# The first feed-forward's input products with output features on the partitions

## The chip, the cores and the metric

The program runs on one core of a Trainium2 chip. The core has a matrix engine (TensorE, in the rows PE for its products and PEld for its weight loads), a vector engine (VectorE, DVE), an activation engine (ScalarE, ACT), GpSimd (POOL) and SyncE (SP), which here only starts transfers. Each engine takes its instructions strictly in the order of the program; engines wait for each other through semaphores. The metric is the device time of one execution in microseconds.

## What is computed

Two transformer blocks on one sequence of 256 tokens, width 2048. The change touches the first block's feed-forward, whose hidden width D_FF is 5632 and whose input product makes 2 x 5632 features. They go through a causal convolution over time with three taps for each feature before the gate is applied:

```python
def rms_norm(x, g):
    xf = x.astype(jnp.float32)
    y = xf * lax.rsqrt(jnp.mean(xf * xf, axis=-1, keepdims=True) + NORM_EPS)
    return (y * g.astype(jnp.float32)).astype(x.dtype)

def conv_glu_ffn(h, w_up, cw, cb, w_down):
    u = causal_depthwise_conv(h @ w_up, cw, cb)      # (256, 2048) @ (2048, 11264), 3 taps
    a, gate = jnp.split(u, 2, axis=-1)
    return (jax.nn.silu(gate) * a) @ w_down

        h = rms_norm(x, ffn_norm_g[l])               # first_block
        x = x + conv_glu_ffn(h, w_up[l], ffn_conv_w[l], ffn_conv_b[l], w_down[l])
```

Around it: the first block's attention with its convolution branch, before; the product with `w_down`, a norm, and the whole second block (two attentions, a gated feed-forward), after.

## The kernel before

All products are float32 in three parts. An operand x is rounded to xh, and the remainder x - xh is xl; a weight gives hi and lo in the same way. A product is xh·hi + xh·lo + xl·hi.

**Items.** The weights come from memory in items of 512 KB: two k-tiles (128 rows each of the contraction) by 512 columns. Each item runs through a pipeline. `load_upto` lets SP start its transfer into a `raw` tile (four of them). `split_upto` (L272) lets ACT round it into `hi` (L281) and DVE subtract it into `lo` (L282); four `hi` and four `lo` tiles exist, `AHEAD` is 3. Then PE uses it. `run_items` writes the program item by item: first the split of the item three places ahead, then this item's products in two halves, one k-tile each. So the instruction `hi` of item i+3 stands on ACT where item i is begun, and it reuses the tile of item i-1.

**Side work.** After each half item `pump` (L242) steps the queues. `urgent` has the rate 0.5: of the functions pushed to it, one is written into the program after every second half, that is one for each item. When a function is written, all its instructions stand on their engines in that place. A function that reads something late therefore holds back whatever stands behind it on the same engine, the splits of later items among it.

**A group** (L201) is all items that make 512 output columns; with a contraction of 2048 it has 8 items. Its mode `xst` (L192) keeps the activations stationary: for each of two halves of the tokens, xh and xl are the weights that PE loads, and 512 columns of hi or lo are the moving operand. The result stands in two PSUM banks, with the tokens on the partitions. An item is 12 products of 512 columns.

**The first feed-forward** is 22 groups: for each of 11 blocks one of the gate columns, one of the up columns. After a group's last product `ffn1_post` (L1045) evicts: `take` copies both banks to `e` tiles on ACT, multiplied by `rstd`, the norm's factor, one for each partition (token). It then pushes for each half b of the 512 features a function `f`: `turn4` transposes four squares of 128 on PE so that features stand on partitions, and `taps3` makes the three taps, the first on ACT (L1036) and four instructions for the other two on DVE (L1041); in a gate group Silu follows (L1055). For an up group a function `g` follows for each half: the product with the gate (DVE, L1061) and the split into `sh` and `sl` for the next product (`split_into`, ACT L418, DVE L419).

**The activations** reach this stage by `turn_split` (L395), which transposes the residual stream and writes xh and xl into separate tiles of the common pool "U" (NU = 63 tiles of 128x512), two k-tiles in each.

Of the kernel before, what the change touches and what calls it, by code (L numbers as in the profile page):

```python
# [17 lines left out]
F32 = mybir.dt.float32  # L18
# [7 lines left out]
P = 128  # L26
# [8 lines left out]
NU = 63  # L35
# [39 lines left out]
class Pipe:  # L75


    def __init__(self):
        self.q = deque()
        self.later = []  # L80
# [26 lines left out]
class Acts:  # L107


    def __init__(self, pipe):  # L110
        self.d = {}
        self.pipe = pipe if callable(pipe) else lambda kt: pipe

# [10 lines left out]
def body(tc, A, out, stop=None, dbg=None):  # L124
# [76 lines left out]
    def group(w, c0, n, kts, X, post, nk=2, before=None, mode=xst, parts=None, tail=None):  # L201
# [33 lines left out]
        for j in range(nch):  # L235
            ld = chunk_loads(w, kts[j * nk], nk, parts or [(c0, n)])
            add(ld, nk * n, mk(j), post=(lambda: post(st["acc"])) if j == nch - 1 else None,
                before=before if j == 0 else None)

# [155 lines left out]
    def turn_split(X, kt, src, c0, gain=None):  # L395

        b = turn4(src, c0)
        hi, lo = U("xh", F32R), U("xl", F32R)
        h, l = two(hi), two(lo)
# [68 lines left out]
    xT = Acts(urgent)  # L468
# [505 lines left out]
    xT2 = Acts(urgent)  # L974
# [54 lines left out]

    def taps3(src, y, f0):  # L1030
# [14 lines left out]
    def ffn1_post(blk, gate):  # L1045
        def post(acc):
            e = take(acc, rstd)
            for b in range(2):
                st = {}

                def f(b=b, st=st):
                    y = st["y"] = U("yf")
                    taps3(turn4(e, b * T), y, (44 if gate else 0) + 4 * blk + 2 * b)
                    if gate:
                        act.activation(y, y, AF.Silu)  # L1055
                        sil[b] = y
                urgent.push(f)

                def g(b=b, st=st):
                    y = st["y"]  # L1060
                    dve.tensor_tensor(y, y, sil.pop(b), op=ALU.mult)  # L1061
                    split_into(hidT, 4 * blk + 2 * b, y)
                if not gate:
                    urgent.push(g)
        return post

    w_up = w2d("w_up")
    for blk in range(11):
        group(w_up, DFF + blk * 512, 512, allk, xT2, ffn1_post(blk, True))
        group(w_up, blk * 512, 512, allk, xT2, ffn1_post(blk, False))  # L1070

    xT3 = Acts(urgent)
# [402 lines left out]
    xT4 = Acts(urgent)  # L1475
# [124 lines left out]
```

## Time and profile before

| | |
|---|---|
| runs of the kernel | 2857.2, 2854.13, 2855.75 us |
| their median | 2855.75 us |
| the profiled execution's own time | 2856.26 us |
| its span, first to last instruction | 2854.5 us |
| PE busy | 2824.9 us, 99% |
| DVE busy | 1636.0 us, 57% |
| ACT busy | 1424.5 us, 50% |
| mean granted clock of TensorE | 0.996 of full speed |

Busy times overlap, since the engines run side by side; idle time of one engine matters only where another waits for it. Matmuls are pipelined: a row's duration is longer than the distance between the starts of neighbours. The stage that the change rewrites lies between about 420 and 923 us of the span.

### The profile page before, as it was taken

What the parts mean: (1) busy time and instruction counts of PE and PEld (TensorE: products, weight loads), DVE (VectorE), ACT (ScalarE), POOL (GpSimd) and SP (SyncE); (2) the same over time, 40 slices, a digit from 0 to 9 for tenths busy, and PEclk for the clock granted to TensorE, in tenths of its full rate; (3) what the DMA queues carried; (4) which work ended last, traced back from release to release, by engine and by line L of the source; (5) the groups of instructions that cost most, each with busy time, mean ns of one, the idle gap of its engine ahead of it and who ended that gap; (6) DMA issues with size and microseconds to landing.
All of it is one profiled execution on the core that took longest, in us unless ns stands there. A gap on an engine that the chain in (4) does not pass through costs nothing.

```text
span 2854.5 us, 34904 instructions
## 1 busy us (share of the span) xinstructions
PE 2824.9 (99%) x13031; PEld 2332.6 (82%) x13031; DVE 1636.0 (57%) x2488; ACT 1424.5 (50%) x2068; POOL 35.7 (1%) x65
## 2 busy tenths in 40 slices
PE   8998999999999999999999999999999999999998
PEld 7886778888888888888888888888888888888887
DVE  6986766666566555565555455555555454554444
ACT  6556555555555444565543555554454444444443
POOL 1201000000000000000000000000000000000000
PEclk9998999999999999999999999999999999999999
DMA  8753336656665566554466655665566666666664
GB/s 233 239 163 106 111 104 185 191 180 191 190 185 188 195 193 196 173 177 121 142 203 195 178 164 169 175 199 188 186 186 189 191 188 190 190 186 195 198 198 159
DMA packets 279578, 513.01 MB, mean 180 GB/s; under 512 B 21222, under 2 KB 46738, under 8 KB 279408
## 3 DMA queue, kind: packets, MB, share of 16 engines
q1 hardware_dynamic: 272256, 502.86, 57.9%
q0 software_dynamic: 4624, 7.13, 0.9%
q8 instruction: 102, 1.67, 0.2%
q10 hardware_dynamic: 2528, 0.79, 0.1%
q14 instruction: 68, 0.56, 0.1%
HBM read 505.45 MB, written 5.24 MB: 179 GB/s over the span
## 4 chain that ended last, share of the span: by engine, by line
PE 97%; DVE 1%; ACT 1%; DMA 0%; issue 0%; SPq 0%; DVEq 0%
PE acc L164 89%; PE tr L391 2%; PE ms L164 1%; PE o L164 1%; PE s L164 1%; DMA raw<-in_w_in 0%; PE ds L164 0%; PE mo L164 0%; PE pt L807 0%; PE do L164 0%; PE hid L164 0%; DVE lo L282 0%; ACT hi L281 0%; PE pt L809 0%; PE pt L808 0%
## 5 line engine op out<-in xcount | busy, mean ns | idle before, releaser
L282 DVE TENSOR_TENSOR lo<-raw,hi 128x1024 fp32r<-128x1024 f32 (+3 forms) x956 | 1153.3, 1211 | 1009.7 <-ACT hi L281 989.0
L281 ACT CAST hi<-raw 128x1024 fp32r<-128x1024 f32 (+3 forms) x956 | 989.8, 1040 | 877.9 <-PE acc L164 817.4
L164 PE MATMUL acc<-hi,xh 128*128 128x512 f32 (+2 forms) x3200 | 1260.7, 394 | 2.0 <-ACT xh L405 2.0
L164 PE MATMUL acc<-hi,xl 128*128 128x512 f32 (+2 forms) x3200 | 1241.3, 388 | 0.5 <-DVE xl L407 0.5
L164 PE MATMUL acc<-lo,xh 128*128 128x512 f32 (+2 forms) x3200 | 1239.5, 387 | 0.0
L164 PEld LDWEIGHTS acc<-hi,xl 128*128 128x128 f32 x3200 | 601.3, 188 | 124.0 <-DVE xl L407 1.0
L164 PEld LDWEIGHTS acc<-hi,xh 128*128 128x128 f32 x3200 | 601.8, 188 | 118.5 <-ACT xh L405 2.3
L164 PEld LDWEIGHTS acc<-lo,xh 128*128 128x128 f32 x3200 | 602.3, 188 | 115.4 <-DVE lo L282 0.5
L164 PE MATMUL acc<-hi,sh 128*128 128x512 f32 x480 | 192.1, 400 | 9.9 <-ACT sh L590 9.9
L164 PE MATMUL acc<-hi,sl 128*128 128x512 f32 x480 | 188.0, 392 | 0.0
L164 PE MATMUL acc<-lo,sh 128*128 128x512 f32 x480 | 187.6, 391 | 0.0
L164 PEld LDWEIGHTS acc<-hi,sh 128*128 128x128 f32 x480 | 90.8, 189 | 27.6 <-ACT sh L590 10.3
L164 PEld LDWEIGHTS acc<-hi,sl 128*128 128x128 f32 x480 | 90.5, 188 | 19.6 <-DVE sl L594 0.2
L164 PEld LDWEIGHTS acc<-lo,sh 128*128 128x128 f32 x480 | 90.9, 189 | 17.6
L526 DVE SCALAR_TENSOR_TENSOR y<-u,cols,y 128x255 f32<-128x255 f32 (+14 forms) x240 | 96.3, 464 | 0.0
L1041 DVE SCALAR_TENSOR_TENSOR yf<-tr,cols,yf 128x254 f32<-128x254 f32 (+1 forms) x176 | 72.6, 475 | 29.3 <-ACT yf L1036 29.3
L1036 ACT ACTIVATE yf<-tr,cols 128x256 f32<-128x256 f32 x88 | 44.8, 560 | 33.7 <-PE tr L391 33.7
L802 ACT ACTIVATE p<-p,mx 128x256 f32<-128x256 f32 x64 | 28.6, 448 | 57.9 <-DVE mx L796 57.9
L164 PE MATMUL acc<-hi,ymh 128*128 128x512 f32 x128 | 49.8, 389 | 0.0
L164 PE MATMUL acc<-lo,ymh 128*128 128x512 f32 x128 | 49.8, 389 | 0.0
L164 PE MATMUL acc<-hi,yml 128*128 128x512 f32 x128 | 49.8, 389 | 0.0
L428 ACT ACTIVATE e<-acc,rstd 128x512 f32<-128x512 f32 x54 | 36.8, 690 | 24.1 <-PE acc L164 24.1
(314 smaller groups left out, 1429.3 us busy)
## 6 DMA issues: line engine op xcount, KB each, us to landing
raw<-in_w_in SPq DMA_DIRECT2D x216, 512.0 KB, 3.7
raw<-in_w_up SPq DMA_DIRECT2D x176, 512.0 KB, 3.9
raw<-in_w_down SPq DMA_DIRECT2D x88, 512.0 KB, 4.7
raw<-in_w_ffn_gate SPq DMA_DIRECT2D x88, 512.0 KB, 4.4
raw<-in_w_ffn_up SPq DMA_DIRECT2D x88, 512.0 KB, 4.0
raw<-in_w_ffn_down SPq DMA_DIRECT2D x88, 512.0 KB, 4.0
raw<-in_w_out SPq DMA_DIRECT2D x64, 512.0 KB, 3.7
raw<-in_w_in SPq DMA_DIRECT2D x64, 256.0 KB, 3.6
```

The lines of the kernel that those rows point to most:

```text
L164: pe.matmul(o, l, r, start=start, stop=stop, skip_group_check=True)
L281: act.copy(it.hi[:, c], it.raw[:, c])
L282: dve.tensor_tensor(it.lo[:, c], it.raw[:, c], it.hi[:, c].bitcast(F32), op=ALU.subtract)
L391: pe.transpose(b[:, kk * T + t * P: kk * T + (t + 1) * P], src[t][:, c:c + P], ident)
L428: act.activation(u[:, :n], acc[t][:, :n], AF.Copy, scale=scale[:, t:t + 1])
L526: dve.scalar_tensor_tensor(y2[:, kk, s:], u2[:, kk, :T - s], w, y2[:, kk, s:], op0=ALU.mult, op1=ALU.add)
L802: act.activation(dst, dst, AF.Exp, bias=nmx, scale=-1.0, accum_out=sums)
L1036: act.activation(y2[:, kk], t2[:, kk], AF.Identity, scale=c(2), bias=col("ffn_conv_b", f))
L1041: dve.scalar_tensor_tensor(y2[:, kk, s:], t2[:, kk, :T - s], col("ffn_conv_w", k * 88 + f), y2[:, kk, s:], op0=ALU.mult, op1=ALU.add)
```

## The change

Only the 22 groups of the first feed-forward get another form, `groupT`. The weights are now stationary: each 128 columns of hi and of lo are loaded into PE, and the activations move. `turn_split` writes xh and xl of a k-tile side by side into one 512-column piece (`X.wide`) of a double tile with a pool of its own (8 of them; NU falls to 47). For hi the moving operand is this piece, xh beside xl, 512 columns; for lo it is xh alone, 256 columns. The output has features on the partitions. It takes four banks, one for each 128 features ("quarter" q): columns 0 to 255 hold hi·xh + lo·xh, columns 256 to 511 hold hi·xl. Groups use two sets of four banks in turn.

The eviction of a quarter stands directly behind its last product: ACT copies the second half of the bank, DVE adds the first. No transposes remain. Since the tokens are now on the free axis, `rstd` is needed as a row for all partitions; `rstd_row` makes it once as `rT`, with a product of `avg` and a diagonal. When both quarters of a half are evicted, a function `f` is pushed: multiply by `rT`, taps, and Silu (gate) or the gate's product with the split (up), all in one function.

```diff
-NU = 63
+NU = 47
...
+    def groupT(w, c0, X, post):
+        st = {}
+        nch = KT // 2
+        par = turn_banks[0] % 2
+        turn_banks[0] += 1
+
+        def mk(j):
+            def f(hi, lo, half):
+                if j == 0 and half == 0:
+                    st["b"] = [psA.tile([P, 512], F32, name=nm("acc"), tag="acc")
+                               for _ in range(4)] if par == 0 else \
+                        [bank("acc") for _ in range(3)] + \
+                        [psO.tile([P, 512], F32, name=nm("acc"), tag="o")]
+                for q in (2 * half, 2 * half + 1):
+                    o = st["b"][q]
+                    for kk in range(2):
+                        kt = 2 * j + kk
+                        c = slice(kk * 512 + q * P, kk * 512 + (q + 1) * P)
+                        xh = X.get(kt)[0]
+                        mm(o, hi[:, c], X.wide[kt], start=j == 0 and kk == 0)
+                        mm(o[:, :T], lo[:, c], xh, stop=j == nch - 1 and kk == 1)
+                    if j == nch - 1:
+                        post(q, o)
+            return f
...
     def turn_split(X, kt, src, c0, gain=None):
...
+            hl = big.tile([P, 1024], F32R, name=nm("hl"), tag="X2", bufs=8)
+            h4 = hl.rearrange("p (k s c) -> p k s c", k=2, s=2)
+            h, l = h4[:, :, 0], h4[:, :, 1]
+            for kk in range(2):
+                X.wide[kt + kk] = hl[:, kk * 512:(kk + 1) * 512]
...
+    def rstd_row():
+        d = U("rd")
+        for t in range(2):
+            dve.tensor_scalar(d[:, t * P:(t + 1) * P], ident, rstd[:, t:t + 1], 1024.0,
+                              op0=ALU.mult, op1=ALU.mult)
+        b = bank("rT")
+        mm(b[:, :T], avg, d[:, :T], start=True, stop=True)
+        act.copy(rT, b[:, :T])
...
     def ffn1_post(blk, gate):
-        def post(acc):
-            e = take(acc, rstd)
-            for b in range(2):
-                st = {}
-
-                def f(b=b, st=st):
-                    y = st["y"] = U("yf")
-                    taps3(turn4(e, b * T), y, (44 if gate else 0) + 4 * blk + 2 * b)
-                    if gate:
-                        act.activation(y, y, AF.Silu)
-                        sil[b] = y
-                urgent.push(f)
-
-                def g(b=b, st=st):
-                    y = st["y"]
+        st = {}
+
+        def post(q, o):
+            if blk == 0 and gate and q == 0:
+                rstd_row()
+            b, kk = divmod(q, 2)
+            if kk == 0:
+                st[b] = U("e")
+            e = two(st[b])
+            act.copy(e[:, kk], o[:, T:])
+            dve.tensor_tensor(e[:, kk], o[:, :T], e[:, kk], op=ALU.add)
+            if kk == 0:
+                return
+
+            def f(b=b):
+                e, y = st.pop(b), U("yf")
+                dve.tensor_tensor(two(e), two(e), rT.unsqueeze(1).broadcast_to([P, 2, T]),
+                                  op=ALU.mult)
+                taps3(e, y, (44 if gate else 0) + 4 * blk + 2 * b)
+                if gate:
+                    act.activation(y, y, AF.Silu)
+                    sil[b] = y
+                else:
                     dve.tensor_tensor(y, y, sil.pop(b), op=ALU.mult)
                     split_into(hidT, 4 * blk + 2 * b, y)
-                if not gate:
-                    urgent.push(g)
+            urgent.push(f)
...
-        group(w_up, DFF + blk * 512, 512, allk, xT2, ffn1_post(blk, True))
-        group(w_up, blk * 512, 512, allk, xT2, ffn1_post(blk, False))
+        groupT(w_up, DFF + blk * 512, xT2, ffn1_post(blk, True))
+        groupT(w_up, blk * 512, xT2, ffn1_post(blk, False))
```

The other `Acts` that are filled by `turn_split` in these shapes (`xT`, `xT3`, `xT4`) are also made with `wide=True`; their groups keep their form.

**The order of ACT and DVE.** ACT before, from the end of an up group: `e` is the eviction, `hi` a weight split, `yf` the taps, `sh` the split of the hidden values.

```order
L428 ACTIVATE e_4647<-acc_4481,rstd 128x512
L428 ACTIVATE e_4649<-acc_4482,rstd 128x512
L281 CAST hi_4651<-raw_4579 128x1024
L1036 ACTIVATE yf_4671<-tr_4672,cols 128x256 x2
L281 CAST hi_4683<-raw_4597 128x1024
L418 CAST sh_4702<-yf_4671 128x512
L281 CAST hi_4706<-raw_4615 128x1024
L1036 ACTIVATE yf_4724<-tr_4725,cols 128x256 x2
L281 CAST hi_4736<-raw_4633 128x1024
L418 CAST sh_4755<-yf_4724 128x512
L281 CAST hi_4759<-raw_4655 128x1024
```

ACT now, the same place; lines are numbered anew, L314 is the weight split.

```order
L1107 COPY e_4756<-acc_4585 128x256
L1107 COPY e_4756<-acc_4586 128x256
L1107 COPY e_4769<-acc_4587 128x256
L1107 COPY e_4769<-acc_4588 128x256
L1088 ACTIVATE yf_4778<-e_4756,cols 128x256 x2
L458 CAST sh_4787<-yf_4778 128x512
L314 CAST hi_4791<-raw_4684 128x1024
L1088 ACTIVATE yf_4817<-e_4769,cols 128x256 x2
L458 CAST sh_4826<-yf_4817 128x512
L314 CAST hi_4830<-raw_4706 128x1024
```

Before, each `yf` and each `sh` had a `hi` in front of it. Now the whole sequence of a half stands between two `hi`, and the first half's directly behind the evictions.

DVE before, at the same group: L1061 is the gate's product, `lo` the weight split.

```order
L282 TENSOR_TENSOR lo_4652<-raw_4579,hi_4651 128x1024
L1041 SCALAR_TENSOR_TENSOR yf_4671<-tr_4672,cols,yf_4671 128x255 x2
L1041 SCALAR_TENSOR_TENSOR yf_4671<-tr_4672,cols,yf_4671 128x254 x2
L282 TENSOR_TENSOR lo_4684<-raw_4597,hi_4683 128x1024
L1061 TENSOR_TENSOR yf_4671<-yf_4671,yf_4495 128x512
L419 TENSOR_TENSOR sl_4703<-yf_4671,sh_4702 128x512
L282 TENSOR_TENSOR lo_4707<-raw_4615,hi_4706 128x1024
L1041 SCALAR_TENSOR_TENSOR yf_4724<-tr_4725,cols,yf_4724 128x255 x2
L1041 SCALAR_TENSOR_TENSOR yf_4724<-tr_4725,cols,yf_4724 128x254 x2
L282 TENSOR_TENSOR lo_4737<-raw_4633,hi_4736 128x1024
L1061 TENSOR_TENSOR yf_4724<-yf_4724,yf_4526 128x512
L419 TENSOR_TENSOR sl_4756<-yf_4724,sh_4755 128x512
```

DVE now, behind the four additions of the eviction; L1114 is the scaling by `rT`, L1121 the gate's product.

```order
L1114 TENSOR_TENSOR e_4756<-e_4756,rT 128x512
L1093 SCALAR_TENSOR_TENSOR yf_4778<-e_4756,cols,yf_4778 128x255 x2
L1093 SCALAR_TENSOR_TENSOR yf_4778<-e_4756,cols,yf_4778 128x254 x2
L1121 TENSOR_TENSOR yf_4778<-yf_4778,yf_4570 128x512
L459 TENSOR_TENSOR sl_4788<-yf_4778,sh_4787 128x512
L315 TENSOR_TENSOR lo_4792<-raw_4684,hi_4791 128x1024
L1114 TENSOR_TENSOR e_4769<-e_4769,rT 128x512
L1093 SCALAR_TENSOR_TENSOR yf_4817<-e_4769,cols,yf_4817 128x255 x2
L1093 SCALAR_TENSOR_TENSOR yf_4817<-e_4769,cols,yf_4817 128x254 x2
L1121 TENSOR_TENSOR yf_4817<-yf_4817,yf_4605 128x512
L459 TENSOR_TENSOR sl_4827<-yf_4817,sh_4826 128x512
L315 TENSOR_TENSOR lo_4831<-raw_4706,hi_4830 128x1024
```

Before, a `lo` stood between the taps and the gate's product of each half. Now everything from the scaling to `sl` stands together for each half, and one `lo` behind it.

PE before, early in the up group: the last three products of a k-tile, a set of transposes (`tr`) of the gate group's `e`, and the next item.

```order
L164 MATMUL acc_4482<-hi_4417,xh_3759 128x512
L164 MATMUL acc_4482<-lo_4418,xh_3759 128x512
L164 MATMUL acc_4482<-hi_4417,xl_3760 128x512
L391 MATMUL tr_4496<-ident,e_4471 128x128
L391 MATMUL tr_4496<-ident,e_4473 128x128
L391 MATMUL tr_4496<-ident,e_4471 128x128
L391 MATMUL tr_4496<-ident,e_4473 128x128
L164 MATMUL acc_4481<-hi_4435,xh_3788 128x512
L164 MATMUL acc_4481<-lo_4436,xh_3788 128x512
```

PE now, in the last item of the first group: the first quarter's last products and the one product for `rT`.

```order
L165 MATMUL acc_3936<-hl_3993,hi_4042 128x512
L165 MATMUL acc_3936<-hl_3993,lo_4043 128x256
L165 MATMUL acc_3936<-hl_3993,hi_4042 128x512
L165 MATMUL acc_3936<-hl_3993,lo_4043 128x256
L165 MATMUL rT_4121<-rd_4118,avg 128x256
L165 MATMUL acc_3937<-hl_3993,hi_4042 128x512
L165 MATMUL acc_3937<-hl_3993,lo_4043 128x256
```

The four transposes are gone; products of 512 and of 256 columns alternate, and `rT` stands once between the first two quarters.

## Rows read from the trace of the kernel before

**Rows 1.** Page: busy us, share of span, instructions; then the chain's shares.

```profile
PE 2824.9 (99%) x13031; PEld 2332.6 (82%) x13031; DVE 1636.0 (57%) x2488; ACT 1424.5 (50%) x2068; POOL 35.7 (1%) x65
...
PE 97%; DVE 1%; ACT 1%; DMA 0%; issue 0%; SPq 0%; DVEq 0%
```

**Rows 2.** Window: us, busy PE PEld DVE ACT POOL, PEclk, DMA share, GB/s.

```profile
425.00:923.00 498.00, 498.00 (x2278) 411.76 (x2277) 307.05 (x394) 273.44 (x354) 0.00 (x0) 1.00 0.61 186
```

**Rows 3.** ACT timeline after gate group: start, duration, operation, count [idle<-releaser].

```profile
489.49 1.04 ACT L281 CAST hi<-raw 128x1024 fp32r<-128x1024 f32 x1
492.07 1.02 ACT L1036 ACTIVATE yf<-tr,cols 128x256 f32<-128x256 f32 x2 [1.53 <-PE tr L391]
494.86 0.63 ACT L1055 ACTIVATE yf<-yf 128x512 f32<-128x512 f32 x1 [1.78 <-DVE yf L1041]
...
499.89 2.93 ACT L281 CAST hi<-raw 128x1024 fp32r<-128x1024 f32 x3
...
519.32 0.62 ACT L418 CAST sh<-yf 128x512 fp32r<-128x512 f32 x1 [2.57 <-DVE yf L1061]
```

**Rows 4.** DVE timeline, the same stretch.

```profile
490.56 1.23 DVE L282 TENSOR_TENSOR lo<-raw,hi 128x1024 fp32r<-128x1024 f32 x1 [2.02 <-ACT hi L281]
493.12 1.65 DVE L1041 SCALAR_TENSOR_TENSOR yf<-tr,cols,yf 128x255 f32<-128x255 f32 x4 [1.33 <-ACT yf L1036]
...
518.55 0.69 DVE L1061 TENSOR_TENSOR yf<-yf,yf 128x512 f32<-128x512 f32 x1
```

**Rows 5.** PE timeline around a transpose of the first feed-forward.

```profile
488.48 0.39 PE L164 MATMUL acc<-hi,xl 128*128 128x512 f32 x1
...
491.20 0.39 PE L164 MATMUL acc<-hi,xl 128*128 128x512 f32 x1
491.43 0.60 PE L391 MATMUL tr<-ident,e 128*128 128x128 f32 x4
...
492.10 0.40 PE L164 MATMUL acc<-lo,xh 128*128 128x512 f32 x1
```

**Rows 6.** PE timeline, 320-column products, first and last of 96.

```profile
1208.14 0.30 PE L164 MATMUL acc<-hi,xh 128*128 128x320 f32 x1
...
1222.07 0.31 PE L164 MATMUL acc<-hi,xl 128*128 128x320 f32 x1
```

**Rows 7.** PE timeline, 256-column products on 48 weight columns, 13 in line.

```profile
84.09 0.28 PE L164 MATMUL acc<-xh,hi 128*48 128x256 f32 x1
...
85.45 0.28 PE L164 MATMUL acc<-xh,hi 128*48 128x256 f32 x1
```

**Rows 8.** Weight loads by form: count, busy us, mean ns, idle before.

```profile
L164 PEld LDWEIGHTS acc<-lo,xh 128*128 128x128 f32 x3200 | 602.3, 188 | 115.4 <-DVE lo L282 0.5
```

**Rows 9.** Tile lnr: count, duration min/median/max ns, first to last start.

```profile
L574 DVE TENSOR_TENSOR y<-y,lnr x8: 418/419/426, 253.2 to 264.2; 128x256 f32<-128x256 f32 x8
...
L569 ACT COPY lnr<-lnr x1: 373/373/373, 252.8 to 252.8; 128x256 f32<-128x256 f32 x1
```

**Rows 10.** Timeline, all engines, start of the first feed-forward.

```profile
419.77 0.47 PE L164 MATMUL acc<-hi,xh 128*128 128x512 f32 x1
...
421.80 1.28 DVE L442 TENSOR_TENSOR xs<-acc,xs 128x512 f32<-128x512 f32 x2
```

**Rows 11.** PE timeline, start of the kernel.

```profile
18.17 0.50 PE L164 MATMUL acc<-hi,xh 128*128 128x512 f32 x1 [2.04 <-ACT xh L405]
...
19.46 0.50 PE L164 MATMUL acc<-hi,xl 128*128 128x512 f32 x1 [0.55 <-DVE xl L407]
```

**Rows 12.** Windows of one-column products and of early waits.

```profile
243.00:250.00 7.00, 7.00 (x25) 5.82 (x25) 4.29 (x14) 3.60 (x5) 1.64 (x3) 0.51 0.34 104
16.00:20.00 4.00, 1.41 (x6) 0.78 (x5) 2.22 (x4) 3.30 (x8) 0.00 (x0) 1.00 1.09 332
```

**Rows 13.** POOL and ACT timelines: one shared tile filled, then copied into.

```profile
227.65 0.52 POOL L921 MEMSET q<- 64x512 f32 x1 [3.21 <-DVE y L526]
...
271.67 1.17 ACT L922 COPY q<-tr 64x512 f32<-64x512 f32 x2
```

More of the change, by code (lines that the diff above doesn't have):

```diff
@@ L107, with __init__ @@
 class Acts:
-    def __init__(self, pipe):
+    def __init__(self, pipe, wide=False):
         self.d = {}
         self.pipe = pipe if callable(pipe) else lambda kt: pipe
+        self.wide = {} if wide else None
     def get(self, kt):
@@ L238, in group @@
                 before=before if j == 0 else None)
+    turn_banks = [0]
+    def groupT(w, c0, X, post):
[21 more added lines that the diff above has]
+            return f
+        for j in range(nch):
+            add(chunk_loads(w, 2 * j, 2, [(c0, 512)]), 1024, mk(j))
     pipes = []
@@ L397, in turn_split @@
         b = turn4(src, c0)
-        hi, lo = U("xh", F32R), U("xl", F32R)
-        h, l = two(hi), two(lo)
+        if X.wide is None:
+            hi, lo = U("xh", F32R), U("xl", F32R)
+            h, l = two(hi), two(lo)
+        else:
[4 more added lines that the diff above has]
+                X.wide[kt + kk] = hl[:, kk * 512:(kk + 1) * 512]
         if gain is None:
@@ L467, in body @@
     x_in = A["x"][0]
-    xT = Acts(urgent)
+    xT = Acts(urgent, wide=True)
     ss1 = small("ss1")
@@ L973, in body @@
     w_out = w2d("w_out")
-    xT2 = Acts(urgent)
+    xT2 = Acts(urgent, wide=True)
     ss2 = small("ss2")
@@ L1028, in body @@
     sil = {}
+    rT = keep.tile([P, T], F32, name="rT")
+    def rstd_row():
[6 more added lines that the diff above has]
+        act.copy(rT, b[:, :T])
     def taps3(src, y, f0):
@@ L1045, in ffn1_post @@
     def ffn1_post(blk, gate):
-        def post(acc):
-            e = take(acc, rstd)
-            for b in range(2):
-                st = {}
-                def f(b=b, st=st):
-                    y = st["y"] = U("yf")
-                    taps3(turn4(e, b * T), y, (44 if gate else 0) + 4 * blk + 2 * b)
-                    if gate:
-                        act.activation(y, y, AF.Silu)
-                        sil[b] = y
-                urgent.push(f)
-                def g(b=b, st=st):
-                    y = st["y"]
+        st = {}
[18 more added lines that the diff above has]
+                    sil[b] = y
+                else:
                     dve.tensor_tensor(y, y, sil.pop(b), op=ALU.mult)
                     split_into(hidT, 4 * blk + 2 * b, y)
-                if not gate:
-                    urgent.push(g)
+            urgent.push(f)
         return post
@@ L1068, in body @@
     for blk in range(11):
-        group(w_up, DFF + blk * 512, 512, allk, xT2, ffn1_post(blk, True))
-        group(w_up, blk * 512, 512, allk, xT2, ffn1_post(blk, False))
-    xT3 = Acts(urgent)
+        groupT(w_up, DFF + blk * 512, xT2, ffn1_post(blk, True))
+        groupT(w_up, blk * 512, xT2, ffn1_post(blk, False))
+    xT3 = Acts(urgent, wide=True)
     ss3, ss4 = small("ss3"), small("ss4")
@@ L1473, in body @@
         group(w_dif, n * 512, 512, allk, ydT, post_dif(n))
-    xT4 = Acts(urgent)
+    xT4 = Acts(urgent, wide=True)
     ss5 = small("ss5")
```

## Prediction

> **What bounds the kernel now.** I read the page's busy times and its chain first, then one window over the first feed-forward, then the timelines of ACT, DVE and PE inside it. TensorE (PE) is busy 99% of the span and the chain that ended last lies 97% on it [rows 1]. So a change counts by what it does to PE's stream, and any other engine counts only where PE comes to wait for it. In the stretch that the change rewrites, 425 to 923 us, PE has no idle time at full clock, while DVE and ACT are busy 307 and 273 of 498 us [rows 2]. By those shares they look like engines with room. The reader should distrust that: share is an average, and both take their work strictly in order. The timeline shows what stands between two weight splits. After a gate group ACT runs `hi` at 489.49, then both taps at 492.07, Silu at 494.86, and not until 499.89 do three `hi` follow without a gap, which is ACT catching up [rows 3]. DVE goes along: `lo` 1.07 us after its `hi`, four taps, `lo` again [rows 4]. PE has four buffers of `hi` and `lo`, so the split of item i+3 can start when item i-1 is done, and PE is covered for three items, some 8 us. Before the change this just suffices.
>
> **The change part by part.**
>
> *Transposes go.* A set of four costs PE what two neighbouring products are held apart: from 491.20 to 492.10 are 0.90 us for two steps. One step is 0.2267, since 488.48 to 491.20 are twelve of them [rows 5]. So a set costs 0.90 - 0.453 = 0.446. Two sets in each of 22 groups are 44: **-19.6 us**, all of it on PE's path.
>
> *Products change shape, not columns.* An item (two k-tiles, 512 features) was twelve products of 512 columns. Now it is eight pairs of one with 512 and one with 256, the same 6144 columns, but sixteen weight loads instead of twelve. The trace has no 256-column product of this type with 128 weight columns. Nearest: 320 columns are 0.1466 apart (95 steps in 13.93 us) [rows 6], against 0.2267 for 512, so 0.000417 a column, and 256 come to 0.1199. From below: 256 columns with only 48 weight columns are 0.1133 apart (12 steps in 1.36 us) [rows 7]. From above I take the 320 spacing itself, 0.1466, as if a shorter product could not hide its load. There are 22 x 8 x 8 = 1408 pairs, each formerly 1.5 x 0.2267 = 0.340. At 0.1200 a pair is 0.3467 and the term is **+9.4 us**; the bounds are 0 and +47. I take 0.1200, since 320 columns are still on the line of 512. An item then takes 8 x 0.3467 = 2.775 us instead of 2.72.
>
> One 128-column load lasts 188 ns in the trace [rows 8], and the products stand 147 to 227 ns apart with such a load for each, so loads do run beside products. The Trainium skill (TensorE: Matmul & The Clock Gate, Part 3: Packing small matmuls — row/col tiling) says that a weight load overlaps running products only when it goes to another row group, and all loads here use all rows. By that rule a 320-column product would stand 188 or more behind its neighbour; the trace disagrees with its 147. The same page (LDWEIGHTS) puts a 128-column load at some 107 ns; one such load laid bare for each 256-column product would make the sum about 150 us longer. I give the rule no share, because the measurement decides.
>
> *The row of 1/rms.* In the last item of the first group, after four of its sixteen products, PE must do one product on two DVE results. These stand on DVE behind `lo` of three items ahead. That `hi` starts with the item, `lo` 1.07 later and takes 1.23 [rows 3, 4], then two small operations of at most 0.42 each, taken from a 128x256 one [rows 9]. So the operand is there about 2.9 us into the item and PE is there at 0.69. A wait of 2.2 and the product: **+2.4 us**, once (1.5 to 3).
>
> *The first group starts on four PSUM banks.* The second half of its first item writes banks that DVE still has to read for the residual (421.80, two in 1.28); the item started at 419.77 [rows 10], its second half 1.39 later, and the first add ends near 422.45. **+1.2 us**, once.
>
> *Eviction and taps, the large term.* Before, the four ACT/DVE sequences of a gate/up pair were stepped after the group's end, behind one further `hi`, and in the up group the halves were split so that a `hi` stood between taps and product. Now (see the order of ACT and DVE under the change) half 0's whole sequence stands before `hi` of item 11 (counting the group's items 0 to 7) and half 1's before `hi` of item 12. Each is a ping-pong: DVE scale, ACT tap, DVE taps, DVE product, ACT rounding. Laid end to end for an up group, from the moment G at which PE starts the next group:
> - last product out at 0.16 (it lasts 0.39 [rows 5]), ACT copy 0.37, DVE add 0.42 [rows 9]: 0.95
> - scale by the row 0.69 (like the 128x512 product [rows 4]), first tap 0.56 (a pair takes 1.02 [rows 3]), four DVE taps 1.65, gate product 0.69 [rows 4], rounding 0.62 [rows 3]: 5.2, where `hi` 11 starts
> - `lo` 11 starts 1.07 later and takes 1.23 [rows 3, 4]: 7.5
> - half 1 again 0.69 + 0.56 + 1.65 + 0.69 + 0.62: 11.7, and with some 0.02 for each of a dozen hand-overs 11.9, where `hi` 12 starts; it ends at 12.95.
>
> PE wants item 12 at 4 x 2.775 = 11.1. It waits 1.85 for `hi`, does one product (0.23), and waits for `lo`, which ends at 11.9 + 1.07 + 1.23 = 14.2, another 1.0: 2.85 us. In a gate group Silu (0.63 [rows 3]) replaces product and rounding in each half: `hi` 11 at 4.5, `lo` 11 done at 6.8, `hi` 12 at 10.45 and done at 11.5, so 0.4 + 1.0 = 1.4 us. Then `hi` 13 to 15 come without a gap and the cover is whole again before the next group ends, so each group pays once. 11 x (2.85 + 1.4) = **+46.8 us**. Where PE waits for weights, the load after the wait lies bare as well: the product behind a wait at the start shows 0.50 instead of 0.39 [rows 5, 11]. 44 waits of 0.11: **+4.8 us**. The term reacts to small things, since it is a difference of 11.9 and 11.1: 0.05 us less at each hand-over take about 12 us off, 0.05 more add as much.
>
> *At nothing.* Sixteen tiles leave the common pool of 63 for a fixed one of eight double tiles. On every engine the instructions up to this stage stand in the same order; what shifts is the wait of POOL's fills and loads for a free tile. The nearest such tile to its use was filled at 227.65 and copied into at 271.67 [rows 13]; some 25 us more of waiting is inside that. Without this cover it would be a wait of that length in the attention. PSUM: a group's four banks are written again only two groups on. DMA is at 0.61 of its time [rows 2]; the bytes are the same.
>
> Sum: -19.6 + 9.4 + 2.4 + 1.2 + 46.8 + 4.8 = **+45 us** on the profiled execution's 2856.26, so 2901. The median of the runs shown lies 0.5 us lower, which changes nothing.
>
> **The rivals.**
> - *The splits keep up* (the other side, faster). If `hi` 12 starts within 10.0 us of G, PE waits nowhere and -19.6 + 9.4 + 2.4 + 1.2 = -6.6 remain: 2850. It decides at 1.9 us less in the two halves together, for instance if DVE's taps ran much quicker from SBUF than from PSUM. For it: PE never waited before, and both engines have 38% idle. Against it: the idle time lies inside the ping-pong and cannot be used by a later `hi`.
> - *Short products bare their loads* (0.1466). The product term is +47, an item 2.99, PE wants item 12 at 11.96, and the waits shrink to about 2.0 and 0.6: 28.6, with 33 bare loads 3.6. -19.6 + 47 + 2.4 + 1.2 + 28.6 + 3.6 = +63: 2920. For it: 256 columns are the first length near a load's own. Against: 320 shows no bend.
> - *The clock falls in the waits.* After PE had done one-column products for 3 us, the clock granted from 243 to 250 was 0.51 [rows 12], the 1.2 GHz level; 7 us at half rate are 3.4 us. If each up group's 3 us of waiting did that: 11 x 3.4 = 37 more, 2938. Against: from 16 to 20, PE waited 2.04 and 0.55 us around one or two products [rows 11] and 1.00 was granted [rows 12].
>
> **How the numbers follow.** Forecast 0.58 (its own range 2886 to 2914, from hand-overs 0.05 off either way), bare loads 0.12, fallen clock 0.13, splits keep up 0.09, and 0.08 for waits of about half the size (2865 to 2885). The range 2878 to 2936 holds the forecast, the bare loads, most of the clock case and the upper part of the half-size waits. Less than 0.2% either way, 5.7 us, is what a measurement of this kernel can't tell from none. Faster is the one rival, 0.09; within 0.2% needs nearly all waits gone but not quite, 0.03, taken from the last 0.08; slower 0.88.
>
> **What would show it.** PE's waits, none in this stretch before, list `acc` waiting for ACT's `hi` and DVE's `lo`, once each per group, in the fifth item of the following group (group items 12), near 1.9 and 1.0 us after up groups and 0.4 and 1.0 after gate groups. The span between neighbouring up groups is about 49 us instead of 45.5. Starts of 256-column products are 0.120 apart from what follows. No transposes between 445 and 925. One wait of PE for DVE's `rd`, near 2 us, about 22 us into the stage. I am wrong if PE stays without waits there, if the waits recur in other items, or if the clock row shows less than full speed.

## The result and the profile after

The changed kernel takes 2924.02 us (median of 4 runs, 2920.6 to 2925.44) against 2855.48 us of the kernel before (4 runs). The ratio is 1.0234, 95% interval 1.0221 to 1.0247: slower by 68.5 us, where the forecast was 45. The profiled execution took 2924.78 us.

The page's busy times and its chain of work, of the changed kernel:

```profile
PE 2845.5 (97%) x13561; PEld 2363.9 (81%) x13561; DVE 1702.3 (58%) x2622; ACT 1431.9 (49%) x2113; POOL 35.8 (1%) x65
...
PE 85%; DVE 8%; ACT 4%; issue 1%; DMA 1%; SPq 0%; ACTq 0%; DVEq 0%
```

PE was 99% busy and 97% of the chain [rows 1]. Now 12% of the chain lie on DVE and ACT: PE waits for them. PE's own busy time grew by only 20.6 us, so most of the loss is waiting. Windows of the changed kernel (columns as in [rows 2]) say where:

```profile
425.00:985.00 560.00, 517.18 (x2818) 442.42 (x2817) 369.89 (x525) 281.32 (x400) 0.00 (x0) 0.97 0.53 165
...
541.70:545.00 3.30, 3.30 (x13) 2.82 (x12) 2.46 (x3) 0.68 (x2) 0.00 (x0) 0.50 0.95 277
...
643.40:648.00 4.60, 4.60 (x28) 4.06 (x27) 3.19 (x4) 1.92 (x2) 0.00 (x0) 1.00 0.91 285
```

The first is the stage: PE is busy 517 of 560 us, where before it had no idle time [rows 2], and the granted clock is 0.97 on average. The second is a stretch that follows a pair of waits: the granted clock is 0.50, the 1.2 GHz level. The third follows an equal pair (1.92 and 0.76 us) at full clock. PE's timeline at the second of these places, in the fifth item behind an up group:

```profile
537.12 0.40 PE L165 MATMUL acc<-hl,hi 128*128 128x512 f32 x1
537.35 0.28 PE L165 MATMUL acc<-hl,lo 128*128 128x256 f32 x1
539.55 0.49 PE L165 MATMUL acc<-hl,hi 128*128 128x512 f32 x1 [1.92 <-ACT hi L314]
540.81 0.39 PE L165 MATMUL acc<-hl,lo 128*128 128x256 f32 x1 [0.77 <-DVE lo L315]
541.03 0.39 PE L165 MATMUL acc<-hl,hi 128*128 128x512 f32 x1
...
541.74 0.63 PE L165 MATMUL acc<-hl,hi 128*128 128x512 f32 x1
542.16 0.42 PE L165 MATMUL acc<-hl,lo 128*128 128x256 f32 x1
542.38 0.63 PE L165 MATMUL acc<-hl,hi 128*128 128x512 f32 x1
```

PE stands still for 1.92 us, does one product and stands for 0.77. A little later its products start 0.42 and 0.22 apart instead of 0.23 and 0.12. ACT's timeline shows what it waited for:

```profile
526.57 0.37 ACT L1107 COPY e<-acc 128x256 f32<-128x256 f32 x1 [0.32 <-PE acc L165]
528.04 1.09 ACT L1088 ACTIVATE yf<-e,cols 128x256 f32<-128x256 f32 x2 [1.09 <-DVE e L1114]
531.24 0.62 ACT L458 CAST sh<-yf 128x512 fp32r<-128x512 f32 x1 [2.11 <-issue]
531.77 1.05 ACT L314 CAST hi<-raw 128x1024 fp32r<-128x1024 f32 x1
534.72 1.10 ACT L1088 ACTIVATE yf<-e,cols 128x256 f32<-128x256 f32 x2 [1.90 <-DVE e L1114]
537.93 0.62 ACT L458 CAST sh<-yf 128x512 fp32r<-128x512 f32 x1 [2.12 <-DVE yf L1121]
538.46 3.89 ACT L314 CAST hi<-raw 128x1024 fp32r<-128x1024 f32 x4
```

DVE in the same stretch:

```profile
527.32 0.68 DVE L1114 TENSOR_TENSOR e<-e,rT 128x512 f32<-128x512 f32 x1
528.67 1.76 DVE L1093 SCALAR_TENSOR_TENSOR yf<-e,cols,yf 128x255 f32<-128x255 f32 x4 [0.67 <-ACT yf L1088]
530.47 0.69 DVE L1121 TENSOR_TENSOR yf<-yf,yf 128x512 f32<-128x512 f32 x1
...
532.85 1.23 DVE L315 TENSOR_TENSOR lo<-raw,hi 128x1024 fp32r<-128x1024 f32 x1 [0.26 <-ACT hi L314]
534.00 0.69 DVE L1114 TENSOR_TENSOR e<-e,rT 128x512 f32<-128x512 f32 x1
...
539.53 4.63 DVE L315 TENSOR_TENSOR lo<-raw,hi 128x1024 fp32r<-128x1024 f32 x4 [0.25 <-ACT hi L314]
```

Read the two side by side: each engine is idle while the other works on the same half. The first half's `hi` starts at 531.77, the second's at 538.46, and `lo` behind it at 539.53. With G = 526.37 (PE wants the fifth item at 537.47, one step of 0.12 behind the product at 537.35; less the 11.1 us of four items) these are G + 5.4, 12.1 and 13.2, where the prediction had 5.2, 11.9 and 13.0. Then four `hi` follow without a gap. Behind gate groups the first wait of the pair is shorter, as PE's timeline shows:

```profile
564.33 0.28 PE L165 MATMUL acc<-hl,lo 128*128 128x256 f32 x1
565.09 0.49 PE L165 MATMUL acc<-hl,hi 128*128 128x512 f32 x1 [0.48 <-ACT hi L314]
566.35 0.39 PE L165 MATMUL acc<-hl,lo 128*128 128x256 f32 x1 [0.77 <-DVE lo L315]
```

The two single waits, for the row of 1/rms in the first group and for its banks:

```profile
443.64 0.28 PE L165 MATMUL acc<-hl,lo 128*128 128x256 f32 x1
445.99 1.06 PE L165 MATMUL rT<-rd,avg 128*128 128x256 f32 x2 [2.07 <-DVE rd L1076]
446.49 0.99 PE L165 MATMUL acc<-hl,hi 128*128 128x512 f32 x1
```

```profile
422.62 0.28 PE L165 MATMUL acc<-hl,lo 128*128 128x256 f32 x1
424.04 0.50 PE L165 MATMUL acc<-hl,hi 128*128 128x512 f32 x1 [1.14 <-DVE xs L482]
```

The kernel before has neither: near the stage's start its trace lists one wait of PE, of 0.21 us.

**The sum, measured.** I took the distance of neighbouring starts on PE all through the stage and set apart those behind a wait. Transposes: -19.6. A pair of products: 0.3485 us on average where there is no wait, against 0.3413 for one and a half products before, times 1408: +10.1. The row: +2.7. The banks: +1.3. The 44 waits behind groups, their bare loads with them: +53.7. A pair costs 3.13 on average behind an up group, and 1.67 behind a gate group where nothing else disturbs it. PE's idle time is 44.1 of the 53.7; the other 9.6, about 0.22 for each wait, is what the product behind it starts later still. Eleven stretches at half clock, ten behind up groups and one behind the row's wait, 1.54 to 1.67 us lost in each: +17.9. Besides, the profiled execution came to this stage 1.5 us later than the one before; it was late from the kernel's start on, where a stretch at half clock stood too. Together +67.6, of 68.5.

### The profile page after: what moved, and what is told of

It reads as the page before. It is cut to its first block, busy times and chain, and to the rows that moved or that the text cites. A ratio compares the mean times of both kernels' runs of the same rounds, so it can differ in the third digit from the quotient of the medians.

```text
span 2923.0 us, 36111 instructions
## 1 busy us (share of the span) xinstructions
PE 2845.5 (97%) x13561; PEld 2363.9 (81%) x13561; DVE 1702.3 (58%) x2622; ACT 1431.9 (49%) x2113; POOL 35.8 (1%) x65
## 4 chain that ended last, share of the span: by engine, by line
PE 85%; DVE 8%; ACT 4%; issue 1%; DMA 1%; SPq 0%; ACTq 0%; DVEq 0%
PE acc L165 78%; DVE lo L315 3%; ACT hi L314 2%; DVE yf L1093 2%; PE tr L424 2%; PE ms L165 1%; PE o L165 1%; DVE e L1114 1%; ACT yf L1088 1%; DVE e L1108 1%; PE s L165 1%; DMA raw<-in_w_in 0%; DVE yf L1121 0%; PE ds L165 0%; PE mo L165 0%
## 5 line engine op out<-in xcount | busy, mean ns | idle before, releaser
L314 ACT CAST hi<-raw 128x1024 fp32r<-128x1024 f32 (+3 forms) x956 | 986.6, 1040 | 927.5 <-PE acc L165 829.2
L165 PE MATMUL acc<-hi,hl 128*128 128x512 f32 (+1 forms) x3456 | 1094.7, 393 | 3.8 <-ACT hl L445 3.2
L165 PEld LDWEIGHTS acc<-hi,hl 128*128 128x128 f32 x3456 | 649.4, 188 | 136.5 <-ACT hl L445 3.5
L165 PE MATMUL acc<-lo,hl 128*128 128x512 f32 (+1 forms) x1728 | 671.6, 389 | 0.0
L165 PE MATMUL acc<-hl,hi 128*128 128x512 f32 (+1 forms) x1440 | 514.9, 401 | 25.9 <-ACT hi L314 24.8
L165 PE MATMUL acc<-hl,lo 128*128 128x256 f32 (+1 forms) x1424 | 407.8, 286 | 16.0 <-DVE lo L315 16.0
L165 PEld LDWEIGHTS acc<-lo,hl 128*128 128x128 f32 x1728 | 325.7, 188 | 63.8 <-DVE lo L315 0.2
L165 PE MATMUL acc<-hi,xh 128*128 128x512 f32 (+1 forms) x768 | 298.9, 389 | 0.0
L165 PEld LDWEIGHTS acc<-hi,xl 128*128 128x128 f32 x768 | 144.2, 188 | 26.6
L165 PEld LDWEIGHTS acc<-hi,xh 128*128 128x128 f32 x768 | 144.3, 188 | 25.9
L165 PEld LDWEIGHTS acc<-lo,xh 128*128 128x128 f32 x768 | 144.4, 188 | 25.4
```

Of the source, the lines that this page charges most:

```text
L165: pe.matmul(o, l, r, start=start, stop=stop, skip_group_check=True)
L314: act.copy(it.hi[:, c], it.raw[:, c])
```

## The experiments

All change the changed kernel, except where it says otherwise. Every time is a median beside runs of the kernel before on the same chip.

**One split more inside an up group's half.**

```diff
-                else:
-                    dve.tensor_tensor(y, y, sil.pop(b), op=ALU.mult)
-                    split_into(hidT, 4 * blk + 2 * b, y)
...
             urgent.push(f)
+
+            def g(b=b):              # gate product and split
...
+            if not gate:
+                urgent.push(g)
```

> The changed kernel, with the gate's product and the split of an up group's half in a function of their own again, so that one weight split more stands inside each half's sequence; gate groups keep theirs. Theory 1 (the undivided sequence of a half between two weight splits makes PE wait): behind up groups the waits of 1.92 and 0.76 us vanish or fall below 0.5, and with them the stretches at the lower clock; behind gate groups 0.5 to 1.0 and 0.8 stay. About 11 x 3.1 + 16 = 50 us less than the changed kernel, less what the gate groups give back: 2870 to 2885 us. Theory 2 (the amount of ACT and DVE work in a group is what PE waits for): the work is the same, so waits of some 50 us in sum stay: 2910 to 2924. Theory 3 (the form of the products costs the time): 2924.

Measured: 2884.04 us, ratio 1.0096 (1.0081 to 1.0111). The groups of PE's products in 425 to 960 us, with the idle time before them:

```profile
L165 PE MATMUL acc<-hl,hi 128*128 128x512 f32 x1396 | 497.4, 400 | 11.9 <-ACT hi L314 11.9
L165 PE MATMUL acc<-hl,lo 128*128 128x256 f32 x1397 | 396.9, 284 | 8.4 <-DVE lo L315 8.4
```

PE waits 20.3 us there. None of the waits is behind an up group. Behind gate groups they grew to 0.55 to 1.75 us for `hi` (0.5 to 1.0 was expected; why they grew more stays open) and are 0.75 to 0.77 for `lo`. Six of these eleven pairs were followed by the lower clock. The work is the same and more than half of the loss is gone (40 of 68.5), so theory 2 and theory 3 fall.

**The sequence in four stages.**

```diff
-            urgent.push(f)
+            urgent.push(f0, f1, f2, f3)   # scale; taps; Silu or product; split
```

> The changed kernel, with each half's sequence cut into four functions (scale; taps; Silu or gate product; split) that are written one item apart, so that a weight split stands behind each. Same instructions in number and kind. Theory 1: no waits behind groups and no lower clock there; left are the one wait for the row of 1/rms with its stretch of lower clock (2.7 + 1.6 us), the first group's wait for banks (1.3), the products (+9.4) and the transposes gone (-19.6): 2855.5 - 4.6 = 2851, within 2848 to 2855. Theory 2: 2910 to 2924. Theory 3: 2924.

Measured: 2856.92 us, ratio 0.9993 (0.9982 to 1.0004). No wait behind any group is left, only the two single ones: theory 1 holds. But the ten runs lie in two clusters, 2847.3 to 2850.5 (four) and 2856.4 to 2859.0 (six). I come back to that.

**Products and eviction alone.**

```diff
             def f(b=b):
-                e, y = st.pop(b), U("yf")
...
+                e = st.pop(b)
+                if not gate:
+                    split_into(hidT, 4 * blk + 2 * b, e)
```

> The changed kernel without the scaling, the taps, Silu and the gate's product: an up group's half is split for the next product as it was evicted, a gate group's half is dropped. This measures products and eviction alone. Theories 1 and 2: no waits behind groups, 2848 to 2855 us as with the sequence in stages; if this is much lower than that kernel, the sequence costs PE something even when it is cut. Theory 3: near 2924, since the products are all there.

Measured: 2853.03 us, ratio 0.9992 (0.9982 to 1.0002), again two clusters (2847.3 to 2850.5 and 2855.5 to 2858.9, five runs each). Taking the taps and all that hangs on them away gains nothing over cutting them into stages: both kernels have the same two clusters, and neither has a wait behind a group.

**Merging alone, in the kernel before.**

```diff
+                    else:            # inside f, behind the taps
+                        dve.tensor_tensor(y, y, sil.pop(b), op=ALU.mult)
+                        split_into(hidT, 4 * blk + 2 * b, y)
                 urgent.push(f)
-
-                def g(b=b, st=st):
-                    y = st["y"]
-                    dve.tensor_tensor(y, y, sil.pop(b), op=ALU.mult)
-                    split_into(hidT, 4 * blk + 2 * b, y)
-                if not gate:
-                    urgent.push(g)
```

> The kernel before, with only the merging of the change: gate product and split of an up group's half stand in one function with the transposes and the taps. Products and eviction as before. If merging alone makes the waits (narrow form of theory 1): waits near 1.9 and 0.8 us behind each up group, 11 x 3.1 + 16 = +50 us: 2905. If it takes the merging together with the longer eviction and the earlier place (wide form of theory 1; here a weight split still stands behind the eviction and before the first half, which puts the second half before the split of item 13 and gives 2.7 us more cover): waits of 0 to 1 us behind up groups and no lower clock: 2855 to 2866. Theory 3: 2855.

Measured: 2859.3 us, ratio 1.0011 (1.0002 to 1.002). The window of [rows 2], in it:

```profile
425.00:923.00 498.00, 497.80 (x2264) 408.37 (x2263) 307.26 (x393) 271.36 (x351) 0.00 (x0) 1.00 0.59 184
```

PE is idle 0.2 us in 498 at full clock. Merging by itself costs 3 us, not 50: behind ten up groups two steps on PE in the sixth item take 0.41 and 0.34 in place of 0.23, some 0.3 us each time. It hurts much only with what the change adds to it, as the wide form of theory 1 has it.

**The place alone.** Both halves' functions one item later, undivided:

```diff
+            if b == 0:
+                urgent.push(None)
             urgent.push(f)
```

> The changed kernel with both halves' functions written one item later, so that one weight split stands behind the evictions and ahead of the first half (the place that they had before the change); each half still undivided. If the place alone makes the waits: they go, and the time is that of the staged kernel, 2845 to 2859. If it takes cutting the sequence: the second half now ends some 14.2 us after the next group's start (two splits of 2.3 on DVE and two sequences of 4.6 to 5.2 in a chain) and hi of item 13 behind it is wanted at 5 x 2.775 = 13.9: waits of 0.3 to 0.9 for hi and 0.8 for lo remain behind every group, few stretches of lower clock: 2880 to 2905.

Measured: 2889.31 us, ratio 1.0115 (1.0101 to 1.0128). PE's products in 425 to 960 us:

```profile
L165 PE MATMUL acc<-hl,hi 128*128 128x512 f32 x1400 | 494.3, 396 | 8.2 <-ACT hi L314 8.2
L165 PE MATMUL acc<-hl,lo 128*128 128x256 f32 x1401 | 396.2, 283 | 13.5 <-DVE lo L315 13.5
```

21.7 us of waiting remain in this window, all in the sixth item behind a group: 0.62 to 0.91 for `hi` and about 0.76 for `lo` behind up groups, 0.23 to 0.76 for `lo` alone behind gate groups (behind the first of them 0.46 for `hi` too). Behind the stage's last group, outside the window, stand 1.97 and 0.76. Three stretches at the lower clock are left, all behind up groups, the last behind the stage's last group. So the place alone doesn't make the waits; it makes about half of the loss (2924.0 to 2889.3), the longer undivided sequence most of the rest (to the staged kernel's 2857).

**A longer sequence in gate groups.**

```diff
                 if gate:
+                    dve.tensor_tensor(y, y, y, op=ALU.max)
                     act.activation(y, y, AF.Silu)
```

> The changed kernel with one more DVE operation of 128x512 (the maximum of the tile with itself, which changes nothing) between taps and Silu of each half of a gate group. If the length of a half's sequence sets the wait (theory 1), the wait for hi behind gate groups grows from 0.48 by two such operations of 0.69 to about 1.9, as behind up groups; the wait for lo stays 0.76: 11 x 1.4 = +15 us. On the clock: if a lower clock follows a wait of that length whichever group makes it, it now comes behind gate groups too, 11 x 1.6 = +18 more, 2957 in all; if something else in the up groups makes it (their split into sh and sl, say), the gate groups keep full speed: 2939.

Measured: 2953.75 us, ratio 1.0342 (1.0323 to 1.0361): +29.7 against the changed kernel. From the starts on PE, waits make +13.8 of it and the lower clock +13.9. The wait for `hi` behind gate groups went from 0.48 to between 1.71 and 2.22 (2.57 behind the first). So the length of a half's sequence sets the wait. Behind these longer waits the clock falls too, though not always; it is the waiting that brings the fall, not something else that up groups do. Windows behind two equal waits (1.93 and 0.75, 1.92 and 0.77 us), both behind gate groups:

```profile
516.90:520.00 3.10, 3.07 (x18) 2.71 (x19) 3.10 (x3) 1.57 (x2) 0.00 (x0) 1.00 0.64 177
...
569.30:572.60 3.30, 3.19 (x11) 2.70 (x12) 3.30 (x4) 1.64 (x2) 0.00 (x0) 0.55 0.60 175
```

Behind the first the clock stays, behind the second it falls to half for most of the 3.3 us. Of this kernel's 22 pairs of waits 19 were followed by a fall (1.70 to 2.57 us for `hi`). Of the changed kernel's 22, it was 10 of the 11 behind up groups (1.71 to 2.63) and none of the 11 behind gate groups (0.26 to 0.78, 1.54 behind the first).

**The row early, and other banks first.** On top of the four stages:

```diff
-            if blk == 0 and gate and q == 0:
-                rstd_row()
+    items[i_ffn1 + 4].before = rstd_diag    # the two DVE operations
+    items[i_ffn1 + 6].before = rstd_row     # product and copy
...
+                    st["b"] = [pa(), pa(), po(), bank("acc")] if first else \
```

> The sequence in four stages, and besides: the row of 1/rms is made in the first group's items 4 and 6, where its operands are ready, and the first group takes two banks that the product before it has not used last. Theory 1: no waits of PE in the stage and no lower clock; against the kernel before: -19.6 (transposes) + 0.5 (the row's product) and the products. If a pair of products takes 0.347 us (+9.4): 2846. If the pair takes 0.3535, as the profile of the staged kernel shows over nearly its whole stage (1408 x 0.0065 = 9.2 more): 2855. Theory P (the alternating stream of 512 and 256 columns has two lasting rhythms, and chance decides which one an execution falls into): times in two clusters 9 us apart. Rival: the two clusters of the staged kernel came from its start or its one wait: one cluster here.

Measured: 2844.69 us, ratio 0.996 (0.9948 to 0.9973), five runs from 2844.4 to 2845.5. That is one cluster, so here the rival came true, and theory P's chance in every execution did not. In the texts that follow, theory P is therefore another one: there are two rhythms, and the wait at the stage's start decides between them. On another chip, beside the staged kernel, once more:

> The staged kernel with the early row of 1/rms and other first banks, once more. Theory P: one cluster at 2845, pairs of 0.347 us. Rival: on a chip where the staged kernel has two clusters, so has this one: 2845 and 2854.

Measured: 2843.98 us, ratio 0.9957 (0.9944 to 0.9969), five runs from 2841.0 to 2846.3, one cluster again. With both of its medians 0.4% below the kernel before, this is the fastest version. The window of its first profile shows no idle time of PE:

```profile
425.00:960.00 535.00, 535.00 (x3020) 468.84 (x3019) 388.79 (x558) 305.99 (x421) 0.00 (x0) 1.00 0.65 191
```

**Two rhythms.** PE's timeline of the staged kernel, in a profiled execution of the upper cluster:

```profile
599.62 0.40 PE L165 MATMUL acc<-hl,hi 128*128 128x512 f32 x1
599.86 0.28 PE L165 MATMUL acc<-hl,lo 128*128 128x256 f32 x1
599.98 0.40 PE L165 MATMUL acc<-hl,hi 128*128 128x512 f32 x1
...
606.69 0.40 PE L165 MATMUL acc<-hl,hi 128*128 128x512 f32 x1
```

The same of the kernel with the early row:

```profile
599.76 0.39 PE L165 MATMUL acc<-hl,hi 128*128 128x512 f32 x1
599.99 0.28 PE L165 MATMUL acc<-hl,lo 128*128 128x256 f32 x1
600.11 0.39 PE L165 MATMUL acc<-hl,hi 128*128 128x512 f32 x1
...
606.70 0.39 PE L165 MATMUL acc<-hl,hi 128*128 128x512 f32 x1
```

From first to last row are 20 pairs: 7.07 us, 0.3535 a pair, against 6.94, 0.347. Nothing waits in either and the clock is full. The slower rhythm holds from 448 us to the stage's end, at 0.352 to 0.353 a pair. The one profile from a lower cluster, of products and eviction alone (2847.3 us), has 0.347 all through. 1408 x 0.0065 = 9.2 us is about the distance of the clusters. In the changed kernel both appear, in stretches between waits. To see what they hang on, the staged kernel ran again beside two others:

> The staged kernel once more, on one chip beside the next two, to see what its two clusters hang on. Theory P (two lasting rhythms of the alternating products, chosen at the wait at the stage's start): clusters near 2848 and 2858 again, while a kernel without that wait shows one. Rival (the chip of that call): one cluster here. The profile should show pairs of 0.347 us in an execution of the lower cluster and 0.3535 in one of the upper.

Measured: 2849.66 us, ratio 0.9984 (0.9975 to 0.9993): six runs from 2846.1 to 2849.7, five from 2854.9 to 2859.1; the profiled one (2859.1) has pairs of 0.353. So the clusters are not a matter of one chip.

> The staged kernel with the early row of 1/rms alone; the first group keeps its banks and its wait of 1.1 us for them. Against the kernel beside it +1.3: 2846 where the pairs take 0.347 us. If the wait for the row chose the rhythm, one cluster; if the wait for the banks does, two, 2846 and 2855.

Measured: 2845.72 us, ratio 0.9964 (0.9951 to 0.9976), one cluster from 2845.1 to 2846.7. It keeps the wait for the banks and loses that for the row, so the clusters come with the wait for the row. With only five runs it is not quite settled: where about half of the runs fall in each cluster, five in the lower one come about once in 30 by chance.

It is tempting to blame the lower clock behind this wait: both profiles of the upper cluster have it (445 to 448 us), and the profile of the lower cluster with this wait has not. Other traces speak against it. In the kernel with both functions one item later the row's wait is followed by full clock, and the slower rhythm sets in all the same:

```profile
445.70:462.00 16.30, 16.30 (x93) 14.12 (x92) 8.86 (x16) 8.63 (x15) 0.00 (x0) 1.00 0.35 98
```

```profile
446.22 0.40 PE L165 MATMUL acc<-hl,hi 128*128 128x512 f32 x1
...
453.28 0.40 PE L165 MATMUL acc<-hl,hi 128*128 128x512 f32 x1
```

These are 20 pairs again, 0.353 each. And in the changed kernel only three of the ten stretches behind a fall within the stage have the slower rhythm. In the kernel with one split more it begins inside an item, at 729 us, where no wait is listed. So the fall is neither needed nor enough. Behind the waits for the row and for splits either rhythm can follow; what decides is not shown.

**Other orders of the products.** Grouped, on the kernel with the early row:

```diff
-                        mm(o, hi[:, c], X.wide[kt], start=j == 0 and kk == 0)
-                        mm(o[:, :T], lo[:, c], xh, stop=j == nch - 1 and kk == 1)
+                    for kk in range(2):
+                        mm(o, hi[:, cc[kk]], X.wide[2 * j + kk], start=j == 0 and kk == 0)
+                    for kk in range(2):
+                        mm(o[:, :T], lo[:, cc[kk]], X.get(2 * j + kk)[0],
+                           stop=j == nch - 1 and kk == 1)
```

> As the kernel beside it, but the four products of a quarter stand as 512, 512, 256, 256 columns instead of 512, 256, 512, 256. Same products and loads. Theory P: the rhythm belongs to the alternation, so one cluster; between 0.340 a pair (the time of its columns, 2836) and 0.347 (2846). Rival (a 256-column product hides its successor's load only partly): two of them in a row lay it bare; with the 0.147 of 320 columns for every second one, 1408/2 x 0.03 = +21: 2867.

Measured: 2847.84 us, ratio 0.997 (0.9959 to 0.9981), one cluster, 2 us above the bounds that I had named. Two steps of 0.233 and two of about 0.115 make 0.348 a pair; loads are not laid bare, and nothing is won.

All of 256 columns (here two quarters share a bank, and what is summed in it is not what the reference sums; the time is that of the instructions):

```diff
+                        mm(o, hi[:, c], xh, start=j == 0 and kk == 0)
+                        mm(o, hi[:, c], xl)
+                        mm(o, lo[:, c], xh, stop=j == nch - 1 and kk == 1)
...
```

> As the staged kernel with the early row, but all products of the stage have 256 columns: hi with xh, hi with xl and lo with xh into the same 256 columns, two quarters in a bank. The eviction is then one DVE operation a half, which also multiplies by the row of 1/rms; ACT's four copies and DVE's four additions of a group go. An item is 24 products. At 0.1133 apart (256 columns on 48 weight columns): 2.72 an item as before, 2855.5 - 19.6 + 0.5 = 2836. At 0.1165 (a 256-column product behind a 512 one in the changed kernel): 2.796, +13.4: 2850. If 256-column products in a row lay part of their loads bare (0.147, the spacing of 320): +141: 2977. Waits of PE: none.

Measured: 2864.55 us, ratio 1.0028 (1.0019 to 1.0038). PE's timeline:

```profile
599.72 0.28 PE L165 MATMUL acc<-hl,lo 128*128 128x256 f32 x1
599.84 0.40 PE L165 MATMUL acc<-hl,hi 128*128 128x256 f32 x2
600.08 0.28 PE L165 MATMUL acc<-hl,lo 128*128 128x256 f32 x1
```

Three products are 0.360 apart, 0.1200 each, between the bounds that I had named and above both favoured values: 2.88 us an item. The simpler eviction can save PE nothing, since no wait behind a group was left.

## Why the prediction was right, and where not

- *What bounds.* Right: PE sets the end, and ACT and DVE, busy about half of the time, came to hold it up by the order of their instructions.
- *Transposes, products, row, banks.* -19.6; +9.4 became +10.1 (0.347 in the faster rhythm, as forecast); +2.4 became +2.7; +1.2 became +1.3. The interpolated 0.1199 for 256 columns is what products of that length take among themselves (0.1200). In a pair, though, the 256 columns took 0.117 and the 512 took 0.230 instead of 0.2267: that the pair came out right to 0.001 is luck. In the row's term the text has a slip: its parts add to at most 3.1 us, not 2.9, so to a wait of at most 2.5; it was 2.07.
- *Eviction and taps.* Right in place, cause and size: the waits stand once a group in the fifth item, for `hi` and then for `lo`. Waits and bare loads were forecast at 51.6 and measured at 53.7. Some luck is in that sum: PE's idle time is 44.1 where 46.8 was forecast, and what a bare load adds is 0.22 for each wait, twice the 0.11 that was read from a row's duration.
- *The clock.* This is the step that failed. The likeliest case had full clock throughout and gave the fall 0.13. It came behind ten of eleven up groups and behind the row's wait, and makes 17.9 of the 23.5 us that the forecast is short. The prediction named a clock row below full speed as a sign that it is wrong, and the row says 0.97. The measured 2924 lies above the likeliest case's own range of 2886 to 2914; the wider range holds it because it took in most of the clock rival. As a rival the fall was priced at 37. One fall costs 1.6 us, not 3.4: it begins about when the second wait ends or later, and lasts some 3.3 us (541.7 to 545.0 above), not 7.

I argued against the fall from two waits at the kernel's start, 2.04 and 0.55 us, behind which full clock was granted [rows 11, rows 12]. One such stretch doesn't show a rule. Below is the stretch behind these waits in the kernel before, then in the kernel with all products of 256 columns, where they are 2.05 and 0.55:

```profile
19.60:22.90 3.30, 3.30 (x17) 2.75 (x18) 2.46 (x5) 3.30 (x8) 0.00 (x0) 1.00 1.02 322
```

```profile
20.20:23.60 3.40, 3.40 (x12) 2.72 (x11) 2.45 (x3) 3.10 (x7) 0.00 (x0) 0.50 0.95 283
```

The waits are equal, and the second pair is followed by half clock. Half clock follows here in 8 of the 14 traces of this case, the changed kernel's among them (3.23 and 0.55).

- *The Trainium skill's rule.* The sentence that the prediction cites from the Trainium skill (TensorE: Matmul & The Clock Gate, Part 3: Packing small matmuls — row/col tiling) has loads overlap only across row groups. With 256-column products 0.12 apart and a 128-column load of some 0.19 us for each, all over all rows, the measurement decides against that sentence here too.
- *Splits keep up.* As a rival it was off in its condition. With `hi` of item 12 starting at G + 10.0, `lo` would end at 12.3, where PE wants it at 11.3: a wait of 1.0 would stay. It takes a start at 9.0, so 2.9 us less and not 1.9. The later place shows such waits for `lo` alone, 0.23 to 0.76. Its time was sound: where the waits are taken away, by cutting the sequence, the staged kernel's lower clusters lie at 2846 to 2850, against the rival's 2850, and with the row early the gain is 10 to 12 us.

## What to carry to other kernels

Where an engine works in order and feeds the bound one, count the longest undivided run of dependent steps between two feeds against the cover in the buffers; the share of busy time says nothing about it. Cut such a run into stages and write one behind each feed: here the same instructions then made PE wait nowhere behind a group (2924 against 2857, and 2845 with the row early and other banks). Price a wait of PE with what may follow it, a stretch at the lower clock, and look for that in more than one place of the trace and in more than one run.

## What the runs showed that was not expected

A stream of alternating 512- and 256-column products has two lasting rhythms, 0.347 and 0.3535 us a pair, at the same granted clock and with no wait; executions of one kernel fall into one or the other and differ by 9 us. What makes the difference inside PE stays open; a fall of the clock is neither needed for it nor enough. And the length of a wait alone doesn't decide whether a fall of the clock follows: pairs of waits with 0.55 to 1.75 us for `hi` had a fall in 6 of 11 cases, those with 1.70 to 2.57 in 19 of 22.
